# Gate products from float32r parts, front banks two and two, and low-rank weights filled up with zeros

## The chip, the cores and the metric

The kernel runs on one core of a Trainium2 chip. Its time is the device time of one execution, in microseconds (us). Before the change it was 1590.78 us, the median of 3 runs (1585.95 to 1590.83). The engines are TensorE (PE, with PEld for its weight loads), VectorE (DVE), ScalarE (ACT), GpSimd (POOL) and SyncE (SP), which issues most transfers.

## The reference

One encoder layer over 256 tokens of width 1024, all in float32. Only what bears on the change is shown.

```python
p = x @ w_in[l]                                   # 1024 x 10560
hq, hf_f, hf_b, hi, hog, prw, gate_a, gate_b = _split(p, IN_SPLITS)
o_a = _hgrn2_branch(hq, hf_f, hf_b, hi, hog, ...)
o_b, v_raw = _rwkv7_branch(prw, ...)              # inside:
#   w = -softplus(-(w0[d] + tanh(wl_d) @ w_up[d])) - 0.5     for d in 0, 1   (64 x 1024 each)
#   a = sigmoid(a0 + a_lo @ a_up)                                            (64 x 1024)
#   then a recurrence over the 256 tokens, forwards and backwards, 16 heads of 64
merged = sigmoid(gate_a) * (o_a @ proj_a[l]) + sigmoid(gate_b) * (o_b @ proj_b[l])
x = _layernorm(DN_ALPHA * x + merged @ w_out[l], ln1_g[l], ln1_b[l])
x = _layernorm(DN_ALPHA * x + _moe(x, ...), ln2_g[l], ln2_b[l])   # 32 experts, top 4, 12 MB each
```

## The kernel before, in words

The program has a front (all up to the first layer norm and the choice of experts) and the experts' stage, which goes through all 32 experts and streams 1 MB pieces of their weights through a ring of tiles.

In the front, the input is loaded and transposed to `X` (channels on partitions, 8 tiles of 256 tokens). `dense_parts` (L129 to L157) makes one 256-column part of a product with a weight matrix: two transfers of 512 rows into a tile `wt` of a pool of three (L136), then for each 128 rows and each half of the columns a matmul of 128x256 into one bank `bank_d` (L154). With a plain moving operand that is 16 float32 products. With a pair of operands (`mov` a tuple) each piece of `wt` is split first (`split`, L112): ScalarE rounds it to float32r (`wh`, L113), VectorE subtracts (`wl`, L114), and three float32r products wh·hi, wl·hi, wh·lo stand for each float32 one. Before the change only the three projections after the branches (proj_b, proj_a, w_out) use pairs.

The branches run in four quarters of 256 columns. Four generators are interleaved by `interleave` (L377) by their running cost: `dense_stream` (the input columns of a quarter, at the end the eight gate parts), `prepare_stream` (`rwkv_prepare`: per quarter the low-rank products L472 and L479, decays, scores L546, and `inverse`), `mix_stream` (the other branch) and `run_stream` (`rwkv_run`: eight steps per quarter, each of which needs the one before: L685, copy `gs`, L696, masked copy into `W`, L710, ScalarE's copy into `W`, L102). `yield ("need", ...)` makes a generator wait until another has reached a point. The tile framework's scheduler then sets the order on each engine, within what the program's order, the banks and the pools allow; each engine works off its own instructions in that order.

The eight banks of the matmul memory are given out by name in L98: three to dense products ("d"), one to preparation ("p"), two to the chain ("c"), one to the mix ("h"), one to outputs ("y").

`gate_part` (L912) makes a gate part with `dense_parts` on `X`, applies a tanh (L916) and calls `fetch` (L955), which issues the next early loads of expert weights once their places are free (`want`, L966). Early loads follow a fixed list, "llsseellpprrrppqqr". The "r" places are four 8 KB slots per partition: `X`, `obT`, `oaT` and one that stays free until the first "r" load. `split_biases` (L283) loads expert biases and splits them on ScalarE and VectorE beside the gate parts.

In a pair of heads (`pair`, L465) the low-rank weights are `wup` (the two directions on partitions 0 to 63 and 64 to 127) and `aup` (64 partitions), loaded once per quarter. Their products contract over 64 partitions.

Of the kernel before, what the change touches and what calls it, by code (L numbers as in the profile page):

```python
# [8 lines left out]
F32 = mybir.dt.float32  # L9
# [7 lines left out]
P = 128  # L17
S = 256
D = 1024
KT = 8  # L20
# [28 lines left out]
def tile_encoder(ctx: ExitStack, tc: tile.TileContext, A, out):  # L49
# [47 lines left out]

    bd, bs, bc, bh, by = (lambda t=t, n=n: bank(t, n) for t, n in (("d", 3), ("p", 1), ("c", 2), ("h", 1), ("y", 1)))  # L98

# [6 lines left out]
    late = ctx.enter_context(tc.tile_pool(name="late", bufs=1, side="right"))  # L106
    X = late.tile([P, KT, S], F32, name="xT0", tag="r", bufs=4)
    obT = late.tile([P, KT, S], F32, name="obT", tag="r", bufs=4)
    oaT = late.tile([P, KT, S], F32, name="oaT", tag="r", bufs=4)
# [209 lines left out]

    lora = fc.tile([P, 3, S], F32, name="lora")  # L320
    b = lora1
    shift(lora[:, 0, :], b[:, :S], "muw")
# [10 lines left out]
    def dense_stream(rw, tmp, hp):  # L333
        for c in range(4):
            yield ("at", c * QUARTER)
            yield ("need", f"pair{c - 1}")
            yield from rwkv_columns(c, rw, tmp)
            yield ("at", c * QUARTER + 45)
            yield ("need", f"mix{c - 1}")
            yield from hgrn_in(c, hp)  # L340
        yield ("at", 4 * QUARTER)
        yield ("need", "pair3")
        for t_ in ("A", "B"):
            g = late.tile([P, 2, 512], F32, name="gate2", tag=t_)
            yield from gate_part(C_GB + (512 if t_ == "B" else 0), [g[:, 0], g[:, 1]])
        yield ("need", "inv3")
        done.add("e")
        for n, t_ in enumerate(("kt", "k0", "sq", "sg")):
            yield from gate_part(C_GA + 256 * n, [tmp.tile([P, 512], F32, name="gate", tag=t_)])
            split_biases(tmp, n)  # L350
        done.add("gates")
# [65 lines left out]
    def rwkv_prepare(qi, rw, tmp):  # L417
# [8 lines left out]
        cq = slice(256 * qi, 256 * qi + 256)  # L426
        wup = tmp.tile([P, 256], F32, name="wup")
        nc.scalar.dma_start(out=wup, in_=A["rw_w_up"][0].rearrange("a l n -> (a l) n")[:, cq])
        aup = tmp.tile([64, 256], F32, name="aup")
        nc.scalar.dma_start(out=aup, in_=A["rw_a_up"][0][:, cq])  # L430
        KB = late.tile([P, 2, 2, S], F32, name="KB", tag="B")
# [33 lines left out]
        def pair(r):  # L465
# [5 lines left out]
            for d in range(2):  # L471
                T.matmul(b[:, d * S:(d + 1) * S], lhsT=wup[64 * d:64 * d + 64, cj],  # L472
                         rhs=lora[64 * d:64 * d + 64, 0, :], start=True, stop=True)
                SC.activation(sg[:, d, :], b[:, d * S:(d + 1) * S], AF.Tanh, scale=0.5,
                              bias=col(hm, "w0", 8 * d + j))
            V.tensor_scalar(sg, sg, 0.5, 0.5, op0=OP.mult, op1=OP.add)
            at = tmp.tile([P, S], F32, name="at")
            b = bs()
            T.matmul(b[:, :S], lhsT=aup[:, cj], rhs=lora[:64, 1, :], start=True, stop=True)  # L479
            sigmoid(at, b[:, :S], col(hm, "a0", j))  # L480
# [431 lines left out]
    def gate_part(w, tiles):  # L912
        for n, g in enumerate(tiles):
            b = yield from dense_parts(w_in, w + 256 * n, X)
            fetch()
            SC.activation(g, b, AF.Tanh, scale=0.5)  # L916
            gates.append(g)
# [37 lines left out]
    def fetch(n=None):  # L955
# [4 lines left out]
        for _ in range(n):  # L960
            i = len(ahead)
            if i >= order.index("b"):
# [3 lines left out]
            want = dict(l="run2" if m < 2 else "run3", s="ring", e="e", p="runs" if m < NA - 2 else "m", q="m",  # L966
                        r=("gates", "gates", "ob", "oa")[m % 4])[k]
            if want not in done:
# [3 lines left out]

    with tc.tile_pool(name="rw", bufs=1) as rw:
        W = rw.tile([P, NW, 2, 4, 64], F32, name="W")
# [510 lines left out]
```

## Time and profile before

| | |
|---|---|
| median of 3 runs | 1590.78 us |
| profiled execution | 1591.12 us (span 1589.3 us) |
| mean granted TensorE clock | 0.981 |
| TensorE busy | 1455.9 us (92% of the span), 11331 matmul records |
| VectorE busy | 591.2 us (37%) |
| ScalarE busy | 374.4 us (24%) |
| transfers | 467.36 MB, 294 GB/s over the span |

The span is one execution from its first to its last instruction; busy times are sums over instructions, and matmul records may overlap. A float32 matmul of this kernel stands as two records of L154 (664 products of the input, 1328 records). The front ends at about 640 us, and the rest is the experts' stage.

### The profile page before, as it was taken

The page shows a single profiled execution, that of the slowest core. Times are in us where ns is not written, and L with a number is a line of the kernel's source. Part 1 is how long each engine was busy: PE and PEld are TensorE (multiplying, and loading weights), DVE is VectorE, ACT ScalarE, POOL GpSimd, SP SyncE. Part 2 cuts the span into 40 slices and gives each one's busy share as a digit, 9 for nine tenths or more (in the row PEclk, how much of TensorE's full clock was granted, in tenths as well). Part 3 has the DMA queues.
Part 4 walks back from the last instruction along what each step waited for, and adds up shares of the span by engine and source line. Part 5 has one row for each costly group of instructions (what it writes and reads, how often), then busy time and mean ns, then how long its engine had stood idle before and what let it go on. Part 6 is the DMA issues. An engine that isn't in the chain of part 4 may idle for free. (4 is left out here: it accounts for less than half of the span.)

```text
span 1589.3 us, 27117 instructions
## 1 busy us (share of the span) xinstructions
PE 1455.9 (92%) x11331; PEld 796.7 (50%) x11331; DVE 591.2 (37%) x1539; ACT 374.4 (24%) x983; POOL 95.0 (6%) x142
## 2 busy tenths in 40 slices
PE   8989989989988999999999999889999988988985
PEld 7667667667666897444444433244434323322321
DVE  4685885985983465112111111121112111111113
ACT  2426335335335243211111111101111100100100
POOL 0310210210210000000000000000000000000000
PEclk9999999999999999999999999989899999999998
DMA  6322322322344786799999999999999999999995
GB/s 190 108 69 68 86 72 67 86 74 70 99 140 134 262 311 241 305 419 415 418 417 416 417 418 416 417 418 416 416 418 418 415 418 417 416 417 418 416 419 208
DMA packets 133981, 467.36 MB, mean 294 GB/s; under 512 B 9544, under 2 KB 66780, under 8 KB 101084
## 3 DMA queue, kind: packets, MB, share of 16 engines
q1 hardware_dynamic: 129280, 460.88, 74.5%
q10 hardware_dynamic: 4572, 4.68, 0.9%
q8 instruction: 91, 1.49, 0.4%
q14 instruction: 38, 0.31, 0.1%
HBM read 464.48 MB, written 1.05 MB: 293 GB/s over the span
## 5 line engine op out<-in xcount | busy, mean ns | idle before, releaser
L154 PE MATMUL bank_d<-xT,wt 128*128 128x256 f32 x1200 | 311.5, 398 | 0.4 <-DMA wt<-in_w_in_dram 0.4
L154 PEld LDWEIGHTS bank_d<-xT,wt 128*128 128x128 f32 x1200 | 217.4, 193 | 39.8 <-issue 6.2
L1238 DVE SCALAR_TENSOR_TENSOR yl<-ypb,slotg,yh 128x512 fp32r<-128x512 f32 x32 | 24.0, 751 | 483.2 <-ACT yh L1237 460.1
L1202 PE MATMUL hpb<-ring_l,xg 128*64 128x512 f32 x416 | 98.7, 602 | 4.7 <-DMA ring_l<-in_moe_w_dram 4.7
L1202 PE MATMUL hpb<-ring_p,xg 128*64 128x512 f32 x416 | 98.5, 598 | 2.4 <-DMA ring_p<-in_moe_w_dram 2.4
L1184 DVE TENSOR_SCALAR ot<-tpb 128x256 fp32r<-128x256 f32 x32 | 13.6, 425 | 233.9 <-ACT tpb L1183 233.9
L1202 PE MATMUL hpb<-ring_r,xg 128*64 128x512 f32 x408 | 96.3, 598 | 4.4 <-DMA ring_r<-in_moe_w_dram 4.4
L1237 ACT ACTIVATE yh<-ypb,slotg 128x512 fp32r<-128x512 f32 x32 | 22.0, 689 | 309.1 <-PE ypb L1232 309.1
L1163 PE MATMUL tpb<-oh,x 128*128 128x256 f32 (+1 forms) x288 | 65.1, 369 | 4.2 <-ACT xg L1168 3.2
L1183 ACT ACTIVATE tpb<-tpb 128x256 f32<-128x256 f32 x32 | 11.8, 370 | 235.3 <-PE tpb L1181 232.1
L1163 PEld LDWEIGHTS tpb<-oh,x 128*128 128x128 f32 x288 | 48.0, 190 | 35.6 <-DVE glu L1214 17.9
L1149 POOL TENSOR_TENSOR ohg<-oh,gate 128x512 f32<-128x512 f32 (+1 forms) x9 | 8.6, 952 | 867.6 <-PE tpb L1181 849.8
L1202 PEld LDWEIGHTS hpb<-ring_l,xg 128*64 128x64 f32 x416 | 29.0, 138 | 56.7 <-issue 40.6
L1202 PEld LDWEIGHTS hpb<-ring_r,xg 128*64 128x64 f32 x408 | 28.1, 136 | 54.7 <-issue 40.2
L1202 PEld LDWEIGHTS hpb<-ring_p,xg 128*64 128x64 f32 x416 | 27.8, 136 | 51.8 <-issue 42.5
L1232 PE MATMUL ypb<-ring_l,aT 128*64 128x512 f32 x208 | 48.8, 597 | 5.0 <-DMA ring_l<-in_moe_w_dram 5.0
L1232 PE MATMUL ypb<-ring_r,aT 128*64 128x512 f32 x200 | 47.3, 598 | 6.4 <-DMA ring_r<-in_moe_w_dram 6.4
L1202 PE MATMUL hpb<-ring_q,xg 128*64 128x512 f32 x200 | 47.2, 597 | 4.5 <-DMA ring_q<-in_moe_w_dram 4.5
L1232 PE MATMUL ypb<-ring_p,aT 128*64 128x512 f32 x192 | 45.0, 599 | 6.9 <-DMA ring_p<-in_moe_w_dram 6.9
L1202 PE MATMUL hpb<-ring_s,xg 128*64 128x512 f32 x208 | 49.2, 598 | 2.2 <-DMA ring_s<-in_moe_w_dram 2.2
L1216 ACT ACTIVATE sgm<-glu 128x256 f32<-128x256 f32 x64 | 26.7, 418 | 102.6 <-DVE glu L1214 102.6
L1202 PE MATMUL hpb<-ring_e,xg 128*64 128x512 f32 x208 | 48.6, 598 | 1.5 <-DMA ring_e<-in_moe_w_dram 1.5
(332 smaller groups left out, 2214.5 us busy)
## 6 DMA issues: line engine op xcount, KB each, us to landing
ring_l<-in_moe_w_dram SPq DMA_DIRECT2D x78, 1024.0 KB
ring_p<-in_moe_w_dram SPq DMA_DIRECT2D x76, 1024.0 KB
ring_r<-in_moe_w_dram SPq DMA_DIRECT2D x76, 1024.0 KB
wt<-in_w_in_dram SPq DMA_DIRECT2D x84, 512.0 KB
ring_s<-in_moe_w_dram SPq DMA_DIRECT2D x40, 1024.0 KB
ring_e<-in_moe_w_dram SPq DMA_DIRECT2D x38, 1024.0 KB
ring_q<-in_moe_w_dram SPq DMA_DIRECT2D x38, 1024.0 KB
ring_b<-in_moe_w_dram SPq DMA_DIRECT2D x38, 1024.0 KB
```

Source lines behind the costliest of these rows:

```text
L154: T.matmul(o, lhsT=lhsT, rhs=rhs, start=n == 0, stop=n == last)
L1149: G.tensor_tensor(out=ohg[:, :, :n], in0=oh[:, :, :n], in1=gate[:, :, es[0]:es[0] + n].unsqueeze(3).to_broadcast([P, 2, n, 64]), op=OP.mult)
L1163: T.matmul(b[:, kk * 256:kk * 256 + ne * 64], lhsT=x1[t][:, n * P:(n + 1) * P], rhs=oh[:, t, :ne].rearrange("p e s -> p (e s)"), start=t = ...
L1183: SC.activation(b[:, :S], b[:, :S], AF.Copy, accum_out=sg)
L1184: V.tensor_scalar(ot, b[:, :S], 0.0, None, op0=OP.is_gt)
L1202: T.matmul(self.hbs[cc][64 * j:64 * j + 64, :], lhsT=self.xg[:, k, self.ei, :], rhs=self.w1[k][:, c0:c0 + 512], start=False, stop=k == KT - 1)
L1216: SC.activation(sgm[cc], glu[cc], AF.Sigmoid, scale=1.702)
L1232: T.matmul(yb[64 * j:64 * j + 64, :], lhsT=self.aT[:, k % 4, 64 * (k // 4):64 * (k // 4) + 64], rhs=self.w2[k][:, j * 512:(j + 1) * 512], ...
L1237: SC.activation(yh, yb, AF.Copy, scale=self.sg)
L1238: V.scalar_tensor_tensor(out=yl, in0=yb, scalar=self.sg, in1=yh.bitcast(F32), op0=OP.mult, op1=OP.subtract)
```

## The change

Four edits, apart from places that follow from them.

1. `X` is split once into `Xh` and `Xl` (float32r), in `dense_stream` after the last pair. `Xh` takes the fourth "r" slot; `Xl` and the weight parts of the gates live in a new pool `gx` (three buffers for the parts). `gate_part` hands the pair to `dense_parts`. The first "r" load now waits for "split" instead of "gates", and takes the slot of `X`.
2. The banks: "d" has two instead of three, "p" two instead of one.
3. The low-rank weights lie in one tile `ups` of 128 partitions, with zeros where a direction or `aup` has no rows, and `lora` has zeros in the unused half; all products contract over 128 partitions. Three transfers per quarter load it.
4. Three memsets at the start write those zeros.

```diff
-    bd, bs, bc, bh, by = (lambda t=t, n=n: bank(t, n) for t, n in (("d", 3), ("p", 1), ("c", 2), ("h", 1), ("y", 1)))
+    bd, bs, bc, bh, by = (lambda t=t, n=n: bank(t, n) for t, n in (("d", 2), ("p", 2), ("c", 2), ("h", 1), ("y", 1)))
...
     X = late.tile([P, KT, S], F32, name="xT0", tag="r", bufs=4)
+    Xh = late.tile([P, KT, S], F32R, name="xh", tag="r", bufs=4)
...
     lora = fc.tile([P, 3, S], F32, name="lora")
+    V.memset(lora[64:128, 1, :], 0.0)
+    ups = fc.tile([P, 3, 256], F32, name="ups")
+    V.memset(ups[64:128, 0:3:2, :], 0.0)
+    V.memset(ups[0:64, 1, :], 0.0)
...
         yield ("need", "pair3")
+
+        Xl = gx.tile([P, KT, S], F32R, name="xl", bufs=1)
+        for k in range(0, KT, 2):
+            split(Xh[:, k:k + 2], Xl[:, k:k + 2], X[:, k:k + 2], V)
+            yield 1
+        box["parts"] = Xh, Xl
+        done.add("split")
...
-        wup = tmp.tile([P, 256], F32, name="wup")
-        nc.scalar.dma_start(out=wup, in_=A["rw_w_up"][0].rearrange("a l n -> (a l) n")[:, cq])
-        aup = tmp.tile([64, 256], F32, name="aup")
-        nc.scalar.dma_start(out=aup, in_=A["rw_a_up"][0][:, cq])
+        for d in range(2):
+            nc.scalar.dma_start(out=ups[64 * d:64 * d + 64, d], in_=A["rw_w_up"][0][d][:, cq])
+        nc.scalar.dma_start(out=ups[0:64, 2], in_=A["rw_a_up"][0][:, cq])
...
-                T.matmul(b[:, d * S:(d + 1) * S], lhsT=wup[64 * d:64 * d + 64, cj],
-                         rhs=lora[64 * d:64 * d + 64, 0, :], start=True, stop=True)
+                T.matmul(b[:, d * S:(d + 1) * S], lhsT=ups[:, d, cj], rhs=lora[:, 0, :], start=True, stop=True)
...
-            T.matmul(b[:, :S], lhsT=aup[:, cj], rhs=lora[:64, 1, :], start=True, stop=True)
+            T.matmul(b[:, :S], lhsT=ups[:, 2, cj], rhs=lora[:, 1, :], start=True, stop=True)
...
-            b = yield from dense_parts(w_in, w + 256 * n, X)
+            b = yield from dense_parts(w_in, w + 256 * n, box["parts"])
...
-                        r=("gates", "gates", "ob", "oa")[m % 4])[k]
+                        r=("split", "gates", "ob", "oa")[m % 4])[k]
...
-    with tc.tile_pool(name="rw", bufs=1) as rw:
+    with tc.tile_pool(name="rw", bufs=1) as rw, tc.tile_pool(name="gx", bufs=3) as gx:
+        hlp[0] = gx
```

Line numbers of the new program are one higher from L112 on (L154 is L155, L195 is L196) and about eleven higher in `rwkv_prepare` and behind it (L472 is L483, L479 is L489, L546 is L556).

The scheduler orders the front anew. TensorE at the start of the program, before: `x_tok` is the input, `prm` the parameter rows, `xT_75` is `X`.

```order
L188 MATMUL bank_d<-ident,x_tok 128x128 x16
L154 MATMUL bank_d<-xT_75,wt 128x256 x24
L195 MATMUL bank_p<-ident,prm 128x116
L154 MATMUL bank_d<-xT_75,wt 128x256 x40
L443 MATMUL bank_p<-blk,sq 128x2 x4
```

And after the change:

```order
L189 MATMUL bank_d<-ident,x_tok 128x128 x12
L196 MATMUL bank_p<-ident,prm 128x116
L189 MATMUL bank_d<-ident,x_tok 128x128 x4
L155 MATMUL bank_d<-xT_75,wt 128x256 x64
L454 MATMUL bank_p<-blk,sq 128x2 x4
```

The transposition of the parameter rows has moved from behind the first 24 products to a place ahead of all of them.

TensorE in the first pair of the first quarter, before: `vT` is transposed, `wup` and `aup` are the low-rank weights, `sqb` and `BK` belong to the same pair.

```order
L461 MATMUL bank_p<-ident,vT 128x128
L154 MATMUL bank_d<-xT_75,wt 128x256 x2
L461 MATMUL bank_p<-ident,vT 128x128 x3
L154 MATMUL bank_d<-xT_75,wt 128x256 x2
L472 MATMUL bank_p<-lora,wup 128x256
L154 MATMUL bank_d<-xT_75,wt 128x256 x2
L472 MATMUL bank_p<-lora,wup 128x256
L154 MATMUL bank_d<-xT_75,wt 128x256 x2
L479 MATMUL bank_p<-lora,aup 128x256
L154 MATMUL bank_d<-xT_75,wt 128x256 x12
```

And after the change:

```order
L472 MATMUL bank_p<-ident,vT 128x128
L483 MATMUL bank_p<-lora,ups 128x256
L155 MATMUL bank_d<-xT_75,wt 128x256
L472 MATMUL bank_p<-ident,vT 128x128 x3
L483 MATMUL bank_p<-lora,ups 128x256
L155 MATMUL bank_d<-xT_75,wt 128x256
L489 MATMUL bank_p<-lora,ups 128x256
L155 MATMUL bank_d<-xT_75,wt 128x256 x9
```

The three low-rank products stand closer together, with one dense product instead of two between them; each still has other work on both sides.

ScalarE in the last steps of the last quarter's chain, before: `W<-bank_c` carries the state to the next step, `W<-vt` writes values, `gate` is a gate part's tanh.

```order
L102 ACTIVATE W<-bank_c 64x2x128 x2
L102 ACTIVATE W<-vt 32x2x64 x4
L916 ACTIVATE gate_5628<-bank_d 128x512
L102 ACTIVATE W<-bank_c 64x2x128 x2
L916 ACTIVATE gate_5628<-bank_d 128x512
L102 ACTIVATE W<-bank_c 64x2x128 x2
L916 ACTIVATE gate<-bank_d 128x512 x3
```

And after the change:

```order
L926 ACTIVATE gate_5778<-bank_d 128x512
L102 ACTIVATE W<-bank_c 64x2x128 x2
L114 ACTIVATE wh<-wt 128x512
L292 ACTIVATE bias<-BK 128x768
L114 ACTIVATE wh<-wt 128x512 x2
L294 ACTIVATE bias<-BK 64x768
L114 ACTIVATE wh<-wt 128x512
L926 ACTIVATE gate_5778<-bank_d 128x512
L114 ACTIVATE wh<-wt 128x512
L102 ACTIVATE W<-bank_c 64x2x128 x2
L114 ACTIVATE wh<-wt 128x512 x3
```

Between two copies of the state ScalarE now has five roundings of weights, and a bias split that stood earlier.

## Rows read from the trace of the kernel before

**Rows 1.** The page's slices of the span: 40 slices of 39.7 us each.
```profile
GB/s 190 108 69 68 86 72 67 86 74 70 99 140 134 262 311 241 305 419 415 418 417 416 417 418 416 417 418 416 416 418 418 415 418 417 416 417 418 416 419 208
```

**Rows 2.** Windows: us; PE, PEld, DVE, ACT, POOL busy (instructions); PEclk, DMA share, GB/s.
```profile
20.00:60.00 40.00, 38.49 (x186) 31.22 (x186) 21.96 (x64) 14.96 (x41) 4.10 (x6) 1.00 0.50 146
180.00:220.00 40.00, 33.21 (x352) 25.88 (x350) 39.11 (x95) 14.04 (x34) 9.44 (x11) 1.00 0.36 102
440.00:500.00 60.00, 47.96 (x865) 36.26 (x854) 42.16 (x105) 27.22 (x85) 8.07 (x13) 0.94 0.45 148
500.00:533.80 33.80, 33.80 (x341) 26.51 (x342) 4.53 (x14) 8.17 (x22) 0.29 (x1) 1.00 0.54 168
533.80:550.60 16.80, 16.80 (x88) 14.99 (x89) 11.26 (x46) 5.35 (x11) 0.00 (x0) 1.00 0.72 254
550.60:640.00 89.40, 84.94 (x660) 78.27 (x660) 53.65 (x118) 36.13 (x61) 0.19 (x1) 0.96 0.79 284
700.00:1570.00 870.00, 809.17 (x4018) 309.26 (x4016) 135.65 (x318) 102.25 (x240) 6.91 (x7) 0.99 1.01 415
```

**Rows 3.** L154 alone: windows of PE; then ns min/median/max, first and last start.
```profile
22.00:37.00 15.00, 15.00 (x71) 1.00 0.61 177
554.00:569.00 15.00, 15.00 (x133) 1.00 0.88 321
...
L154 PE MATMUL bank_d<-xT,wt x1200: 379/379/796, 9.1 to 548.7; 128*128 128x256 f32 x172
L154 PE MATMUL bank_d<-obh,wh x64: 276/276/365, 550.6 to 574.3; 128*128 128x256 f32 x64
```

**Rows 4.** Timeline of PE: start us, us, instruction; two stretches.
```profile
47.57 0.70 PE L472 MATMUL bank_p<-lora,wup 64*128 64x256 f32 x2
48.19 1.13 PE L154 MATMUL bank_d<-xT,wt 128*128 128x256 f32 x4
49.25 0.70 PE L472 MATMUL bank_p<-lora,wup 64*128 64x256 f32 x2
...
542.86 0.60 PE L741 MATMUL bank_c<-lora,gup 128*128 128x256 f32 x2
543.29 1.46 PE L154 MATMUL bank_d<-xT,wt 128*128 128x256 f32 x6
544.59 0.59 PE L741 MATMUL bank_c<-lora,gup 128*128 128x256 f32 x2
```

**Rows 5.** Timeline of PE and ACT's queue at the start; ACT's queue from 10 to 11.
```profile
6.05 3.17 PE L188 MATMUL bank_d<-ident,x_tok 128*128 128x128 f32 x15 [1.04 <-DMA x_tok<-in_x_dram]
9.06 10.54 PE L154 MATMUL bank_d<-xT,wt 128*128 128x256 f32 x48
19.43 0.26 PE L195 MATMUL bank_p<-ident,prm 116*128 116x116 f32 x1
20.12 1.10 PE L154 MATMUL bank_d<-xT,wt 128*128 128x256 f32 x4 [0.42 <-DMA wt<-in_w_in_dram]
...
9.74 0.28 ACTq L182 DMA_DIRECT2D prm<-in_ln_b_dram  x1
...
q10 hardware_dynamic: 12, 0.00, 1.4%
```

**Rows 6.** Groups (busy us, mean ns); waits to 620 us (total, times, longest); PE's timeline.
```profile
L113 ACT ACTIVATE wh<-wt 128x512 fp32r<-128x512 f32 x48 | 29.2, 629 | 32.3 <-PE bank_d L154 14.4 <-DMA wt<-in_proj_a_dram 10.7 <-DMA wt<-in_w_out_dram 3.2
L114 DVE TENSOR_TENSOR wl<-wt,wh 128x512 fp32r<-128x512 f32 x48 | 31.9, 687 | 15.8 <-ACT wh L113 15.8
...
ACT bias L291 <- DMA BK<-in_moe_b_dram: 23.2, 4, 8.0
ACT wh L113 <- DMA wt<-in_proj_a_dram: 10.7, 8, 3.2
PE bank_p L546 <- DVE L L553: 5.1, 4, 1.6
...
450.67 0.66 PE L827 MATMUL bank_h<-QQ,KS 128*32 128x32 f32 x32 [3.84 <-ACT KS L102]
```

## The prediction

> **What bounds the kernel now.** I read first the page's slices [rows 1]: from the 18th slice on, at 675 us, the DMA rate stands at 415 to 419 GB/s until the last slice. That is the experts' stage, which streams the expert weights. The view by windows gives the same for 700 to 1570 us: DMA share 1.01, 415 GB/s, TensorE 809 of 870 us [rows 2]. Nothing there is changed, the loads keep their order, and only a fixed list of them is fetched early. So this stage starts when the front has ended, takes as long as before, and a microsecond gained or lost ahead of 640 us moves the end by one microsecond.
>
> The front is then read window by window [rows 2]. From 20 to 60 us TensorE works 38.5 of 40 us, VectorE 22. From 180 to 220 us, where a quarter's pairs and inverse stand, VectorE works 39.1 of 40 and TensorE only 33.2. From 440 to 500 us no engine is full (TensorE 48.0 of 60, VectorE 42.2, ScalarE 27.2): steps wait for each other. From 500 to 550.6 us TensorE is busy without a gap (33.8 of 33.8 and 16.8 of 16.8), with the last steps of the recurrent chain and the gate products between them. From 550.6 to 640 it works 84.9 of 89.4 on the three projections. So work taken from TensorE counts in the first and in the fourth of these stretches, and is hidden in the second.
>
> **The change part by part.**
>
> *Gate products.* The eight gate parts hold 16 products of 128x256 each, 128 in all. A float32 product stands as two records. In 15 us of nothing but these the windows count 71 records of 0.379 us [rows 3]; records that reach over an edge count too, so the spacing is (15 + 0.379)/71 = 0.2166 us and a product 0.433. The projections already use float32r parts: 133 records of 0.276 us in 15 us, (15 + 0.276)/133 = 0.1149 us each. Three of them make a gate product: 0.345 us. The change gives back 128 x (0.433 - 0.345) = 11.3 us of TensorE's time. In the new order a step of the last chain has 48 float32r records beside it (5.5 us) where three quarters of a gate part stood (12 products, 5.2 us). The steps thus stay about as long, but each takes a whole gate part along, and 132 records (15.2 us) are left behind the chain's last output instead of 32 products (13.9 us). The saving must therefore appear in the stretch before that output. I take it whole, since TensorE is the full engine there.
>
> What it adds lies on ScalarE and VectorE: 4 + 32 roundings of 128x512 on ScalarE (0.629 us each, 22.6 us) and as many subtractions on VectorE (0.687 us, 24.7 us) [rows 6]. From 440 to 550.6 us these two are busy for 40.7 and 58.0 of 110.6 us [rows 2], so they fit. The four splits of x are placed by the order in the second quarter, far from need. The risk is the queue: the roundings stand on ScalarE between the copies that carry the state from step to step. Bounds: if the x split and the first gate part stood in series in the path, 8 x 0.629 + 8 x 0.687 = +10.5 us; if the new order took away all of TensorE's idle time from 440 to 500 us, -12.0. I take 0, by the nearest row: after 500 us TensorE waits for nothing.
>
> *Low-rank products.* Wup and aup products (24: 16 and 8) use 64 rows of the array. Such a product takes 47.57 to 48.19 = 0.62 us, and the four records behind it 48.19 to 49.25 = 1.06 us, where 4 x 0.2166 = 0.87 would do [rows 4]. A 128-row product of the same columns, from 542.86 to 543.29, takes 0.43, and the six records behind it 1.30, exactly 6 x 0.2166. So a 64-row product costs 0.19 + 0.19 = 0.38 us more than a filled one, 24 of them 9.1 us. The Trainium skill ("TensorEngine Tiling (Array Packing)", Key Properties) says that changing the tiling mode drains TensorE; the rows agree, with 0.38 us per pair of changes. The same notes ("TensorE: Matmul & The Clock Gate", Why this matters for your kernels) advise the opposite for small contractions: slices at different partitions, so that they run at once. By that rule the filled form would lose 0.43 us per pair of directions, 0.9 us in the first quarter, and the sum would be 1581.5; the rows show the two products 1.7 us apart, so no such overlap is there to lose. Six of the 24 lie in the first quarter, where TensorE is full: -2.3 us. The other 18 lie where VectorE is full; the nearest row is 180 to 220 us, and I take 0 for them. Bounds: 0 and -9.1. The three memsets stand before the first x arrives and cost nothing.
>
> *The start.* Before, the transposition of the parameter rows (L195) stood behind the first 24 products. In the new order it stands ahead of the last four transpositions of x, and so ahead of all products, because the second "p" bank is free. It waits for 15 small transfers. The last is issued at 9.74 us [rows 5]; in the window from 10 to 11 us twelve packets of that queue still move. I estimate its landing at 11.8 us, between 11 and 13. Then follow 0.26 us for it and 4 x 0.21 for the transpositions, and products start at 12.9 instead of 9.06: +3.8. The pause from 19.43 to 20.12 goes: -0.7. Net +3.1, bounds 0 and +5. From 20 to 60 us TensorE is the full engine [rows 2], so its lateness is passed on.
>
> *Banks two and two.* TensorE's waits for a reader of the single "p" bank sum to 5.1 us in the largest row [rows 6], and that is the most to win. With two "d" banks instead of three, a product may run only one product (6.9 us) ahead of its reader; ScalarE stands up to 8.0 us in four waits for the bias transfers (23.2 us in all) [rows 6], so up to 4 x 1.1 = 4.4 us could be lost. TensorE's 3.84 us of idle time ahead of L827 at 450.67 come from ScalarE, late in this way. I take 0.
>
> **Sum.** -11.3 - 2.3 + 3.1 = -10.5 us. The profiled execution took 1591.1 us (span 1589.3), 0.3 above the median of the runs, so 1580.6, told as 1580.5.
>
> **The rivals.**
> 1. *The drain counts everywhere* (the rule named above, taken in full). If TensorE is late in all quarters, because what VectorE waits for comes from it, the other 18 low-rank products count too: -6.8 more, 1573.8. For it: in each pair VectorE's work comes behind these products. Against: VectorE's 39.1 of 40 us [rows 2].
> 2. *The chain is the bound.* If the last chain keeps its length from 440 to 533.8 us, since its copies now share ScalarE with roundings, then only the 32 products left behind it shrink, by 32 x 0.088 = 2.8 us: 1591.1 - 2.8 - 2.3 + 3.1 = 1589.1. For it: the stretch from 440 to 500, where no engine is full. Against: from 500 us on TensorE has no gap.
> 3. *ScalarE waits for weights, with the chain behind it: slower.* A rounding needs its weight tile, and ScalarE works in order. In the projections such waits are 10.7 us in 8 [rows 6], 1.34 each, and cover nothing but the next rounding. With the gates, 16 tiles come this way, and state copies stand behind them; if each wait is passed on, +21.4 us: 1602. It outweighs the gain from 0.66 us per tile on. For it: the DMA share there is 0.54 to 0.72, with expert loads in the same queue. Against: three tiles are in flight, and a tile now comes free after the split, not after the product.
>
> **How the numbers follow.** Forecast 0.50 (1575 to 1586), rival 1 0.15, rival 2 0.22, rival 3 0.13. The measurement can tell 0.3%, 4.8 us, so faster means below 1586.0 and slower above 1595.6. Faster: 0.50 + 0.15 + 0.03 of rival 2 = 0.68. Slower: 0.10 of rival 3. Same: 0.22. The range 1571 to 1592 holds the forecast, most of rival 1 and rival 2, and leaves rival 3 out; it covers the open terms of the start and of the banks.
>
> **What would show it.** In the new profile: the first product at about 13 us; gate records spaced 0.115 us; low-rank products of 128 rows with 0.43 us to the next record; the first projection product about 10 us earlier than 550.6; the same 415 GB/s after that. Wrong would be: ScalarE waiting for the weight transfers or for bias transfers ahead of state copies, with TensorE idle from 500 to 540 us; or larger gaps in the middle quarters.

## The result, and the profile after

The changed kernel takes 1570.12 us, the median of 4 runs (1567.42 to 1573.84), beside 1590.8 us for the kernel before: a ratio of 0.9876 with a 95% interval of 0.9844 to 0.9908, or -19.7 us (-24.8 to -14.6). The forecast was -10.5. The direction held; the gain is twice as large, the median lies 0.9 us below the low end of the range (by the ratio it is 1571.1, at its very edge), and most of it does not come from where I had looked for it. The span of the profiled execution is 1569.9 us.

The experts' stage is as it was. The page's slices, clock above and rate below, to be held against [rows 1]:

```profile
PEclk9999999999999999999999999989899999999998
GB/s 168 98 78 81 86 74 81 100 59 82 110 123 198 289 293 219 386 415 417 419 415 416 418 417 415 418 417 415 418 417 416 417 418 418 415 418 417 416 419 211
```

415 to 419 GB/s again from the 18th slice on, and the 17th has 386 where it had 305. From the start of the last group of router products (L1065; L1054 before) to the end it took 959.6 us before and 957.3 now. So the front has to be read. The windows of the kernel after, in the columns of [rows 2], the last two cut at the first projection product (535.3 us; 550.6 before):

```profile
20.00:60.00 40.00, 38.81 (x193) 32.45 (x191) 18.35 (x50) 15.14 (x41) 0.49 (x1) 1.00 0.51 145
180.00:220.00 40.00, 35.47 (x576) 28.52 (x575) 38.77 (x115) 14.80 (x36) 6.43 (x9) 0.96 0.29 84
440.00:500.00 60.00, 50.07 (x776) 43.14 (x774) 38.61 (x95) 39.15 (x112) 7.97 (x13) 0.91 0.43 141
500.00:535.30 35.30, 34.47 (x341) 32.76 (x341) 23.69 (x68) 16.91 (x31) 0.19 (x1) 0.95 0.82 274
535.30:612.60 77.30, 74.20 (x618) 72.37 (x617) 49.69 (x89) 33.30 (x56) 0.00 (x0) 0.98 0.74 260
```

TensorE is still not full from 440 to 500 us, it has gaps from 500 us on where it had none, and the granted clock is 0.91 and 0.95 where it was 0.94 and 1.00. The gate products, the part from which I expected most, run in the stretch that looks worse than before.

A fixed window compares different work in two kernels. Cut at events of the program instead (the first low-rank product of a quarter, the first projection product, the last group of router products), the profiled executions divide like this. "Work" is TensorE's busy time less what the lower clock cost, "clock" is that cost (in windows of 1 us, the sum of one minus the granted clock), "idle" the rest of the stretch, "turns" the number of places in TensorE's timeline where two neighbouring records have different rows*columns of the array:

| kernel | to quarter 1 | quarters 1 to 3 = work + clock + idle (turns) | quarter 4 to first projection = work + clock + idle | projections |
|---|---|---|---|---|
| before | 47.6 | 342.2 = 305.8 + 8.5 + 27.9 (295) | 160.8 = 141.4 + 3.4 + 16.0 | 79.1 |
| zeros only | 48.8 | 334.5 = 300.3 + 6.8 + 27.4 (266) | 163.0 = 139.7 + 6.8 + 16.5 | 79.5 |
| gates only | 47.9 | 339.5 = 306.2 + 6.8 + 26.5 (297) | 162.4 = 129.8 + 12.3 + 20.3 | 76.8 |
| dense banks only | 54.1 | 342.0 = 305.7 + 8.5 + 27.8 (295) | 164.0 = 141.1 + 5.1 + 17.8 | 79.9 |
| banks only | 51.3 | 325.1 = 299.6 + 1.7 + 23.8 (257) | 153.0 = 142.4 + 0.0 + 10.6 | 83.4 |
| banks and zeros | 52.7 | 325.8 = 296.8 + 5.1 + 23.9 (240) | 152.7 = 141.2 + 3.4 + 8.1 | 79.1 |
| full change | 51.2 | 327.7 = 297.2 + 10.2 + 20.3 (244) | 156.5 = 132.4 + 8.8 + 15.2 | 77.3 |

(The five in the middle are experiments, below. Each row is one profiled execution.) Of the 19.4 us by which the span fell, 14.5 come from quarters 1 to 3, 4.3 from the fourth with the gates, 1.8 from the projections and 2.3 from the rest; 3.6 are lost at the start.

The places that the prediction named, after. The start (TensorE's timeline; compare [rows 5]):

```profile
12.51 0.43 PE L196 MATMUL bank_p<-ident,prm 116*128 116x116 f32 x1 [3.79 <-DMA rwt<-in_router_w_dram]
12.73 1.06 PE L189 MATMUL bank_d<-ident,x_tok 128*128 128x128 f32 x4
```

Products start at 13.59 us (forecast about 13). The low-rank products, now of 128 rows (compare [rows 4]):

```profile
51.17 0.60 PE L483 MATMUL bank_p<-lora,ups 128*128 128x256 f32 x2
51.61 0.59 PE L155 MATMUL bank_d<-xT,wt 128*128 128x256 f32 x2
52.07 0.55 PE L472 MATMUL bank_p<-ident,vT 128*128 128x128 f32 x3
52.45 0.60 PE L483 MATMUL bank_p<-lora,ups 128*128 128x256 f32 x2
52.89 0.59 PE L155 MATMUL bank_d<-xT,wt 128*128 128x256 f32 x2
```

51.17 to 51.61 is 0.44 us (forecast 0.43, before 0.62). And gate records, 21 of them from one of these rows to the other:

```profile
476.01 0.28 PE L155 MATMUL bank_d<-xl,wh 128*128 128x256 f32 x1
...
478.51 0.28 PE L155 MATMUL bank_d<-xl,wh 128*128 128x256 f32 x1
```

(478.51 - 476.01)/21 = 0.119 us each (forecast 0.115). So every price of a single operation was right. What was wrong is where they count.

### The profile page after: what moved, and what is told of

The parts are those of the page before. It is cut to its first block, busy times and chain, and to the rows that moved or that the text cites. A ratio compares the mean times of both kernels' runs of the same rounds, so it can differ in the third digit from the quotient of the medians.

```text
span 1569.9 us, 27470 instructions
## 1 busy us (share of the span) xinstructions
PE 1441.8 (92%) x11459; PEld 806.8 (51%) x11459; DVE 602.1 (38%) x1578; ACT 395.1 (25%) x1019; POOL 90.2 (6%) x142
## 5 line engine op out<-in xcount | busy, mean ns | idle before, releaser
L155 PE MATMUL bank_d<-xT,wt 128*128 128x256 f32 x944 | 238.7, 395 | 0.4 <-ACT pad L102 0.4
L155 PEld LDWEIGHTS bank_d<-xT,wt 128*128 128x128 f32 x944 | 173.5, 193 | 27.9 <-issue 1.5
L115 DVE TENSOR_TENSOR wl<-wt,wh 128x512 fp32r<-128x512 f32 x80 | 54.1, 688 | 33.2 <-ACT wh L114 31.6
L1174 PEld LDWEIGHTS tpb<-oh,x 128*128 128x128 f32 x288 | 48.0, 190 | 35.5 <-DVE glu L1225 17.8
L114 ACT ACTIVATE wh<-wt 128x512 fp32r<-128x512 f32 x80 | 48.9, 628 | 46.9 <-PE bank_d L155 26.3
L1213 PEld LDWEIGHTS hpb<-ring_r,xg 128*64 128x64 f32 x408 | 28.1, 137 | 54.7 <-issue 40.2
L1213 PEld LDWEIGHTS hpb<-ring_p,xg 128*64 128x64 f32 x416 | 27.9, 137 | 51.4 <-issue 42.5
L1243 PE MATMUL ypb<-ring_l,aT 128*64 128x512 f32 x208 | 48.8, 597 | 4.9 <-DMA ring_l<-in_moe_w_dram 4.9
```

The source lines that it names most:

```text
L114: SC.activation(hi, src, AF.Copy)
L115: eng.tensor_tensor(out=lo, in0=src, in1=hi.bitcast(F32), op=OP.subtract)
L155: T.matmul(o, lhsT=lhsT, rhs=rhs, start=n == 0, stop=n == last)
L1174: T.matmul(b[:, kk * 256:kk * 256 + ne * 64], lhsT=x1[t][:, n * P:(n + 1) * P], rhs=oh[:, t, :ne].rearrange("p e s -> p (e s)"), start=t = ...
L1213: T.matmul(self.hbs[cc][64 * j:64 * j + 64, :], lhsT=self.xg[:, k, self.ei, :], rhs=self.w1[k][:, c0:c0 + 512], start=False, stop=k == KT - 1)
L1243: T.matmul(yb[64 * j:64 * j + 64, :], lhsT=self.aT[:, k % 4, 64 * (k // 4):64 * (k // 4) + 64], rhs=self.w2[k][:, j * 512:(j + 1) * 512], ...
```

## Experiments

All are compared with the kernel before by the ratio of runs on the same chip in the same session. The us behind a ratio are worked out from it and that session's median of before.

**Zeros alone.** Only edits 3 and 4. The order on TensorE stays the same, row for row.

```diff
-                T.matmul(..., lhsT=wup[64 * d:64 * d + 64, cj], rhs=lora[64 * d:64 * d + 64, 0, :], ...)
+                T.matmul(..., lhsT=ups[:, d, cj], rhs=lora[:, 0, :], ...)
...
-            T.matmul(b[:, :S], lhsT=aup[:, cj], rhs=lora[:64, 1, :], ...)
+            T.matmul(b[:, :S], lhsT=ups[:, 2, cj], rhs=lora[:, 1, :], ...)
```

> The kernel before, with only the low-rank weights and inputs filled up to 128 rows. Every engine keeps its order of work. Theory A (the prediction's): only the 6 products of the first quarter count, 6 x 0.38 = -2.3 us, 1588.5. Theory B (rival 1: the cost of the 64-row form counts in all quarters): 24 x 0.38 = -9.1 us, 1581.7. B is also what the two profiles suggest, where TensorE's busy time in each middle quarter fell by 2.4 to 3.2 us.

Measured: 1583.14 us, ratio 0.9964 (0.9942 to 0.9987), -5.7 us (-9.2 to -2.1). TensorE's work in quarters 1 to 3 fell by 5.5 us, and by 1.7 in the fourth: 7.2 for 24 products, 0.30 each where I had 0.38. B is right in that they count in all quarters. The 29 turns that went are 0.19 us each.

**Gates alone.** Only edit 1.

```diff
-            b = yield from dense_parts(w_in, w + 256 * n, X)
+            b = yield from dense_parts(w_in, w + 256 * n, box["parts"])
```

> The kernel before, with only the gate products from float32r parts (and X split). Theory A (the prediction's): 128 x 0.088 = -11.3 us, 1579.5, gained ahead of the first projection product. Theory C (the chain of the last quarter is the bound, as in rival 2): only what stands behind the chain shrinks, -2.8 us, 1588. The profile of the full change points to C: from the fourth quarter's first low-rank product to the first projection product it took 156.5 us against 160.8, and 2.3 of these 4.3 are owed to the low-rank products.

Measured: 1583.33 us, ratio 0.9957 (0.9940 to 0.9975), -6.8 us (-9.5 to -4.0): between the two. But the stretch with the gates did not get shorter: 162.4 us against 160.8. Work fell by 11.6 there, as forecast, and came back as 8.9 of clock and 4.3 of idle time. In this execution what was gained lies elsewhere: 2.7 in quarters 1 to 3, 2.3 in the projections, 3.0 behind them; why was not tested. The granted clocks of all runs say the same of the clock: 0.978 on average in these 12 runs, 0.982 in the 23 of the kernel before. Span times one minus the clock makes that 34.1 and 28.2 us lost; what is left of the span fell by 12.2 us.

**Banks alone.** Only edit 2.

```diff
-... (("d", 3), ("p", 1), ("c", 2), ("h", 1), ("y", 1)))
+... (("d", 2), ("p", 2), ("c", 2), ("h", 1), ("y", 1)))
```

> The kernel before, with only two banks each for the dense products and for preparation. Theory A (the prediction's): the start is 3.1 us later and the rest even, 1594. Theory D (the second preparation bank takes away TensorE's idle time in the middle quarters): the start 4 us later, and about 3.6 us of idle time gained in each of the second and third quarters as in the profile of the full change, so -3 us, 1587.5.

Measured: 1573.66 us, ratio 0.9897 (0.9872 to 0.9923), -16.4 us (-20.3 to -12.2). The term that I had put at 0 is the largest of all, and outside its bounds. Theory D has the right part and too small a price. The windows over quarters 1 to 3 (first low-rank product to the fourth quarter's first), before and then with the banks alone:

```profile
47.57:389.80 342.23, 314.31 (x4382) 235.41 (x4381) 259.53 (x689) 151.39 (x464) 60.42 (x79) 0.98 0.28 78
```

```profile
51.32:376.41 325.09, 301.30 (x4354) 232.37 (x4353) 249.57 (x690) 150.37 (x462) 57.43 (x79) 0.99 0.29 83
```

TensorE is busy for 13 us less with the same work to do (the records differ by 28, at the cuts), and that is the surprise: three quarters of the gain are not gaps that closed but busy time that went. Of these 13 us, 6.8 are clock; how far that holds for other runs is told in the part on the prediction.

**Start mended.** The changed kernel, with one line more:

```diff
     for k in range(0, KT, 2):
-        b = bd()
+        b = bd() if k < 4 else bc()
```

> The changed kernel, with the last two groups of transpositions of x in the chain's banks instead of the dense ones, so that the first two dense banks are not waited for and the transposition of the parameter rows stands behind the first 24 products again, as before. Theory A (the start's lateness is passed on to the end): products start at 9.1 instead of 13.6 us and the end comes about 4 us earlier than in the changed kernel, 1566. Theory E (the first quarter's later waits take the lateness up): within 1 us of the changed kernel, 1570.

Measured: 1570.01 us, ratio 0.9867 (0.9839 to 0.9895): no difference from the changed kernel that this can tell. Products start at 9.26 us, and yet the first low-rank product comes at 50.79 instead of 51.17. A row of TensorE's timeline shows where the 4.3 us went:

```profile
23.96 19.22 PE L155 MATMUL bank_d<-xT,wt 128*128 128x256 f32 x80 [3.34 <-ACT sh_t L309]
```

TensorE stands for 3.34 us until ScalarE has read the first of the two dense banks; that read needs a value out of the parameter rows, whose transposition is now late again. The granted clock is 0.57 from 24 to 28 us, behind this pause. With two dense banks the parameter rows are waited for either way, before the products or between them. So theory E holds, though what takes the lateness up is the pair of dense banks, not a wait in the first quarter.

**One preparation bank, two dense banks.** This splits the bank edit.

```diff
-... (("d", 3), ("p", 1), ...
+... (("d", 2), ("p", 1), ...
```

> The kernel before with two dense banks instead of three and one preparation bank as before (one bank stays unused). Theory H (the second preparation bank brings all of the gain, the lost dense bank costs the start): products start at 13.6 us and the end is about 4 us later than before, 1592. Theory I (fewer dense products ahead of their readers leave fillers for the stretches where TensorE is idle): faster than before by 5 us or more, below 1583.

Measured: 1597.67 us, ratio 1.0036 (1.0022 to 1.0050), +5.7 us. Theory H: the lost dense bank costs 5.7 us (in the profile the first low-rank product is 6.5 us late), and the second preparation bank is worth the difference to the kernel with both, 0.9897 - 1.0036, about -22 us. The transposition of the parameter rows moves ahead of the products in this kernel too, which has one "p" bank.

**Banks and zeros.** The full change less the gates' edit (the diff of the gates alone, undone).

> The changed kernel without its first edit: gate products in float32 again, banks two and two, low-rank weights filled up. Theory A (each part keeps its own gain): 1588.5 - 16.4 (banks only) - 5.4 (zeros only) = 1567 and the gates' 5.2 on top would have made the full change 1562; as that was 1570, at least one gain is lost in company. Theory F (the gates' gain is lost once the chain is short: ScalarE's bias splits wait for their transfers inside the chain, VectorE's state copies stand behind them): 1567 to 1569, not slower than the full change. Theory G (the low-rank gain is lost with two preparation banks): 1573, as banks only, and the gates bring 3.

Measured: 1570.18 us, ratio 0.9861 (0.9839 to 0.9884), -22.1 us. The full change has 0.9876 (0.9844 to 0.9908). So in this company the gates' edit gives nothing that can be measured, and the profile says why: 8.8 us less work in its stretch, 5.4 more of clock and 7.1 more of idle time, 156.5 us against 152.7. Whether the zeros still count beside two "p" banks is not settled: the ratios of this and of banks alone have overlapping intervals, and the 2.8 us of work that went from quarters 1 to 3 came back as clock. The nine profiled kernels with both, here and below, take 324.9 to 327.7 us for quarters 1 to 3, and banks alone takes 325.1, so nothing in that stretch shows that they do.

**Where TensorE waits in the gates' stretch.** No run of its own, but the reading on which the next ones rest. Timelines of the full change from 492 to 501 us, ScalarE first, then VectorE, then TensorE, and the windows behind them:

```profile
497.28 0.84 ACT L292 ACTIVATE bias<-BK 128x768 bf16<-128x768 f32 x1 [5.17 <-DMA BK<-in_moe_b_dram]
```

```profile
498.16 0.96 DVE L293 TENSOR_TENSOR BK<-BK,bias 128x768 f32<-128x768 f32 x1 [5.32 <-ACT bias L292]
499.03 0.68 DVE L115 TENSOR_TENSOR wl<-wt,wh 128x512 fp32r<-128x512 f32 x1
499.64 0.28 DVE L104 COPY gs<-bank_c 128x128 f32<-128x128 f32 x1
```

```profile
499.98 0.43 PE L706 MATMUL bank_c<-gs,Y 32*32 32x64 f32 x16 [3.53 <-DVE gs L104]
```

```profile
492.00:501.00 9.00, 5.47 (x70) 4.95 (x70) 3.50 (x6) 3.47 (x6) 0.00 (x0) 1.00 0.34 89
501.00:505.00 4.00, 4.00 (x44) 3.49 (x43) 2.55 (x5) 1.82 (x4) 0.00 (x0) 0.57 0.59 163
```

Read upwards: TensorE waits 3.53 us for the chain's `gs`. VectorE could have copied it at 494.8, when L695 (494.39) had ended, but stood at L293 for the bias group, because ScalarE stood at L292 for the transfer. TensorE was idle for 3.53 of the 9 us, and in the next one the granted clock is 0.57, so it is at 1.2 GHz for most of it. This was theory F; rival J held the splits of the gate weights themselves guilty.

**Bias loads early.**

```diff
+        fgs = [load_biases(BK, 0), load_biases(f12[:, :768], 1), load_biases(f12[:, 768:1536], 2)]
         for n, t_ in enumerate(("kt", "k0", "sq", "sg")):
             yield from gate_part(...)
-            split_biases(tmp, n)
+            split_biases(fgs[n], n)
+            if n == 0: fgs.append(load_biases(BK, 3))
```

> The changed kernel with the four bias loads issued ahead of the last four gate parts, into tiles that are free by then, instead of one after each part into one tile; the splits stay. Theory F (the waits for bias transfers in the chain, 5.2 and 2.1 us on ScalarE, make TensorE idle for 8.8 us and then run at the lower clock): the stretch from the fourth quarter's first low-rank product to the first projection product falls from 156.5 to about 148, the end to 1562. Rival J (the roundings and subtractions themselves delay the state's copies): 155 to 157, the end within 2 us of the changed kernel.

Measured: 1574.47 us, ratio 0.9894 (0.9876 to 0.9911): no better than the full change, and both theories missed (the stretch took 159.5 us). The scheduler, seeing the data early, moved the splits early too, into the stretch where VectorE is full: ScalarE waited for the transfers there (17.6 us in 3 waits), the first chain step of the last quarter came at 458.2 us instead of 445.0, with half the clock from 450 to 464. The late steps did become short (the state's copies on ScalarE 5.8 to 8.2 us apart, against 10.8 and 12.9 in the full change). Inconclusive on the cause.

**The same, with the subtractions on GpSimd.**

```diff
-                    split(wh, wl, wq, V)
+                    split(wh, wl, wq, G if hlp[0] is box.get("gx") else V)
```

> As the kernel with early bias loads, and the subtractions of the gates' weight parts on GpSimd instead of VectorE (32 of 128x512). Theory F: VectorE is not what is late once the bias waits are gone: within 3 us of that kernel, 1560 to 1565. Rival J: VectorE's 32 x 0.69 = 22 us leave the queue of the state's copies, 5 us or more faster than that kernel. If GpSimd takes much longer for one than VectorE's 0.69 us, the float32r products wait for it and the run is slower than 1568.

Measured: 1573.93 us, ratio 0.9894 (0.9872 to 0.9915): as the kernel above, within the 3 us of theory F, though both are far from its 1560. VectorE had 32 instructions less and the end did not move. Its busy time in the stretch fell by 9.3 us only (119.8 to 110.5), where 22 had been expected, and one subtraction took GpSimd 1.32 us:

```profile
L115 POOL TENSOR_TENSOR wl<-wt,wh 128x512 fp32r<-128x512 f32 x32 | 41.9, 1319 | 46.9 <-ACT wh L114 40.7 <-issue 3.4 <-PE bank_c L714 1.9
```

(The view of groups by line: busy us and mean ns of one, then the idle time ahead of them.)

**Bias loads and splits behind the chain** (with the mended start):

```diff
                 b = dense(wp, 256 * g, (hi, lo))
+                if g % 2 == 0: fg = load_biases(mg, 2 * which + g // 2)
+                else: split_biases(fg, 2 * which + g // 2)
```

> The kernel with the mended start, and the four bias loads and splits moved behind the chain, beside the first two projections (a tile of a pool that opens there). So nothing on ScalarE or VectorE waits for a bias transfer while the chain runs. Theory F (the bias waits in the chain ate the gates' gain): the stretch from the fourth quarter's first low-rank product to the first projection product falls from 156.4 to 147 to 149 us, the projections take 1 us more, the end is at 1562. Rival J (the roundings and subtractions themselves delay the chain's copies): the stretch stays at 155 or more, the end at 1569.

Measured: 1582.34 us, ratio 0.9947 (0.9931 to 0.9962). The end is worse, but the stretch in question speaks against rival J: with the waits gone from the chain, quarter 4 to the first projection takes 144.2 us, against 156.3 in the kernel with the mended start, with the same splits of weights on the same engines and no lower clock at all. The work of the bias splits left the stretch too (0.84 us for each of two roundings and 0.96 for each of two subtractions in a group), so the run shows the price of waits and bias splits together; that the waits are the larger part is read from the timelines above. Two windows, up to the first projection product and from there to the router:

```profile
376.79:520.98 144.19, 135.21 (x1946) 114.39 (x1944) 112.10 (x305) 74.71 (x194) 19.69 (x28) 1.00 0.51 162
520.98:621.78 100.80, 81.43 (x618) 78.08 (x617) 56.43 (x97) 39.55 (x64) 0.00 (x0) 0.90 0.66 216
```

The 12 us gained and 11 more are lost in the projections, where the waits now stand (view of waits, 500 to 625 us; total, times, longest):

```profile
ACT bias L295 <- DMA fg<-in_moe_b_dram: 28.5, 4, 10.3
DVE fg L296 <- ACT bias L295: 26.1, 4, 10.2
...
PE bank_d L155 <- ACT wh L114: 14.1, 3, 8.4
```

My "1 us more" for the projections was wrong by 22: ScalarE waits up to 10.3 us for a bias transfer there, beside the expert loads, and roundings stand behind it.

**The same, with float32 gates** (the diff of the gates alone, undone in the kernel above).

> As the run before, with the gate products in float32 again. Theory F: the gates' parts are worth 4 to 8 us once the bias waits are gone, so this is slower than the run before, 1566 to 1570. Rival J: the gates' parts bring nothing or cost 2 to 4 us in any company, so this is equal or faster, 1562 to 1566.

Measured: 1594.52 us, ratio 1.0025 (1.0011 to 1.0038), slower by 12 us. In the profiled executions, 16.5 us apart, the larger part is the projections (113.7 us against 100.8), where the bias waits meet this kernel harder; in the stretch with the gates it is 149.8 against 144.2. So without bias waits in the chain the gates' parts are worth 5.6 us there: 6.7 of work and 1.7 of clock less, 2.8 of idle time more. That is theory F in the stretch; its time for the whole kernel, like J's, was far off. Held against the kernels with the biases in the chain, moving them shortened the stretch by 12.1 us with float32r gates (156.3 to 144.2) and by 2.9 with float32 ones (152.7 in banks and zeros, whose start is another, to 149.8).

**Splits left out.** The reverse test of rival J.

```diff
-                    wh, wl = new tiles; split(wh, wl, wq, V)
+                    if len(hlp) > 1: wh, wl = hlp[1]
+                    else: ...; split(wh, wl, wq, V); hlp.append((wh, wl))
```

> The changed kernel with 31 of the 32 splits of gate weights left out: all gate products use the parts of the first piece, so the gates' values are not the reference's. TensorE's products and their order of magnitude stay, ScalarE and VectorE are spared 31 x 0.63 and 31 x 0.69 us, and the bias waits stay in the chain. Rival J: the stretch from the fourth quarter's first low-rank product to the first projection product falls from 156.5 to 148 or less, 1562. Theory F: 153 to 156, 1567 to 1570.

Measured: 1577.91 us, ratio 0.9917 (0.9899 to 0.9934), slower than the full change by its ratio (0.9876), though the intervals touch. The stretch took 163.4 us, 7 more than with the splits. That misses both numbers, and J by its sign. The view of waits, 370 to 545 us:

```profile
ACT bias L297 <- DMA BK<-in_moe_b_dram: 23.6, 4, 10.5
...
PE bank_c L700 <- ACT W L102: 9.6, 1, 9.6
...
PE bank_c L669 <- ACT Z L102: 5.4, 1, 5.4
```

ScalarE, relieved of the roundings, waited longer for the bias transfers (23.6 us in 4 waits, 13.0 in the full change), with the state's copies behind it. Timelines of ScalarE and its queue tell whether it came sooner or the transfers later. The last group, issue and end of the wait, with the splits left out:

```profile
478.06 1.14 ACTq L295 DMA_DIRECT2D BK<-in_moe_b_dram  x2
493.83 0.84 ACT L297 ACTIVATE bias<-BK 128x768 bf16<-128x768 f32 x1 [10.45 <-DMA BK<-in_moe_b_dram]
```

In the full change the issue that belongs to the wait of 5.17 us shown above:

```profile
488.31 1.10 ACTq L290 DMA_DIRECT2D BK<-in_moe_b_dram  x2
```

From the issue to the end of the wait it is 15.8 us against 9.0, and ScalarE began to wait 5.3 us behind the issue against 3.8. So it did not come sooner; the transfers landed later, while the core moved 297 GB/s (478 to 494 us) against 143 (488 to 498 us). That the other loads held them up is not shown. As the waits grew, this run is no clean test of J.

**Loads early, splits held late.** The version to which this points: the three loads early as above, and each split tied on ScalarE behind the tanh of its gate part, so that the scheduler can't pull it forward.

```diff
-            split_biases(fgs[n], n)
+            with tc.issue_after(last[0].ins):     # last[0]: the part's tanh
+                split_biases(fgs[n], n)
```

> The changed kernel with the mended start, the first three bias loads issued early (as in the kernel with early bias loads) and each split held behind the tanh of one of the last four gate parts, so that it stands behind the chain's last copy on ScalarE and its data has long landed; the fourth load follows the first split. Theory F (the bias waits ate the gates' gain in the chain, and moved along with the splits in the two kernels that shifted them): the fourth quarter's first low-rank product to the first projection product takes 144 to 147 us as in the kernel with late biases, the projections 77 to 80 as in the changed kernel, the end is at 1557 to 1561, faster than all others. Rival K (the fourth transfer lands late and ScalarE waits with roundings behind it): 4 to 8 us more, 1563 to 1567. Rival J (the splits of weights are what delays the chain): 155 us for that stretch, 1568.

Measured: 1565.44 us, ratio 0.9847 (0.9823 to 0.9872), -24.3 us (-28.1 to -20.3). It has the lowest ratio of all kernels run, though its interval overlaps that of the full change. No wait for a bias transfer is left in the front. Three windows: quarter 4 to the chain's last output, from there to the first projection product, the projections:

```profile
376.50:498.33 121.83, 115.21 (x1758) 94.50 (x1756) 95.20 (x249) 63.31 (x175) 19.48 (x27) 0.99 0.47 146
498.33:527.98 29.65, 24.85 (x190) 23.19 (x189) 21.40 (x61) 14.31 (x25) 0.19 (x1) 0.88 0.65 221
527.98:606.43 78.45, 75.96 (x616) 74.11 (x616) 53.77 (x93) 37.04 (x61) 0.00 (x0) 0.98 0.75 266
```

The first took 134.2 us in the full change, so 12.4 us are gained. The second took 22.3, so 7.4 are given back: the four splits now stand between the last gate parts' roundings, and TensorE is idle for 4.8 us of that stretch and at the lower clock for part of it (0.88). Theory F's 144 to 147 us came out as 151.5, its 1557 to 1561 as 1565. That lies in rival K's 1563 to 1567, but the late fourth transfer that K names is not in the trace.

## Why the prediction was right, and where it was wrong

*What bounds the kernel.* Right: the experts' stage kept its length within 2.3 us, and the front's gain arrived at the end.

*Banks two and two: taken as 0, bounds -5.1 to +4.4; measured -16.4.* This is the step that failed. I bounded the second "p" bank by TensorE's waits for a reader of the single one, 5.1 us in the largest row [rows 6], "and that is the most to win". It was not even all of these waits: the same view has another row for a reader of that bank.

```profile
PE bank_p L546 <- DVE bon L492: 3.2, 4, 1.1
```

Neither row is left in banks only. And such a row counts only the time in which TensorE stood at that bank. It leaves out what the scheduler does so that TensorE won't stand there: with one bank it puts dense products between two preparation products. Each such place is two turns, for which I had a price in hand (0.38 us per pair, from [rows 4]) and which I applied to 24 products instead of to every turn in the order. In quarters 1 to 3 the second bank (dense banks only against banks only) takes 16.9 us away: 6.1 of work for 38 fewer turns, 0.16 each; 6.8 of clock; 4.0 of idle time (the clock's part does not hold over the runs, see below). The other half of the edit I had nearly right: the lost dense bank costs 5.7 us, with a bound of 4.4.

The Trainium skill ("TensorEngine Tiling (Array Packing)", Key Properties) says that a change of tiling mode drains TensorE. The runs agree, with 0.16 to 0.19 us of work per turn. The Trainium skill ("TensorE: Matmul & The Clock Gate", A second HAM failure mode: psum-queue depth-cycling) describes a kernel whose short pauses at its banks bring the lower clock. The runs do not show that of these banks: in quarters 1 to 3 the clock cost 6.8 to 8.5 us in the four profiled kernels with one preparation bank, and 1.7 to 10.2, 6.3 on average, in the ten with two.

*Low-rank products: taken as -2.3; measured -5.7 alone.* The size per product was near (0.30 us for 0.38), the place was wrong. "The other 18 lie where VectorE is full", and I took 0 for them: they counted, as rival 1 said, at least in the kernel without the other edits. VectorE's 39.1 of 40 us hold in the window that I chose, but over quarters 1 to 3 it is busy for 259.5 of 342.2 us, and TensorE for 314.3. I read a whole quarter from its fullest 40 us.

*Gate products: taken as -11.3, whole.* The work that went is 8.8 to 11.6 us, as forecast. The step that failed is "I take it whole, since TensorE is the full engine there", and with it, for the splits, "I take 0, by the nearest row". The prediction's own sign of error, ScalarE waiting for bias transfers ahead of state copies, is what came: I had counted 23.2 us of these waits before, and used them for the banks alone. They cost less beside float32 gate products: with their splits they are worth 2.9 us of the stretch there and 12.1 beside float32r ones. In the full change they reach the chain through VectorE's queue, and its gates' stretch is 3.8 us longer than with float32 gates: 7.1 of idle time and 5.4 of clock more, 8.8 of work less. Without them the edit is worth 5.6 us there, half of what I took.

*The start: taken as +3.1.* First product at 13.59 us, 3.6 us late at the first low-rank product: the size was right. The reason that I gave ("because the second p bank is free") was wrong: the order moves with two dense banks and one "p" bank just as well, and mending it doesn't bring the time back.

*The sum.* -10.5 came out as -19.7 because one term at 0 was -16 and the gates' term did not arrive. Alone the three parts give -16.4, -5.7 and -6.8, together -28.9, and in company -19.7. Banks and zeros together measured -22.1, as much as their two alone, so it is the gates' part that shows no gain in company. That the direction held and the time came to the edge of the range is luck: the largest term failed, and one that was put at nothing stood in for it.

*The rivals.* Rival 1 (1573.8) named a true mechanism and came nearest in time, with the banks' part, the largest, not in it. Rival 2 (the chain bounds the gates' stretch) was right about that stretch. Rival 3 had the queue right, ScalarE waiting with state copies behind it, and the wrong transfer: biases, not weights.

That fewer turns, less idle time and a higher clock together make the 16.9 us is read from single profiled executions. For the clock every run has its granted mean: span times one minus that mean is 25.2 us on average in the six runs of banks only and 28.2 in the 23 of the kernel before, 3.0 apart. In the two profiled executions it is 20.4 (0.987 over 1570.8 us) and 30.2 (0.981 over 1589.3 us). So the clock's 6.8 is in good part the luck of one execution; without the clock the mean span fell by 12.4 us.

## What to carry to other kernels

Price a change of banks by the order that it lets the scheduler make, not by the waits that the trace shows at the bank: count the places where the array's shape turns, before and after, and give each its price. Here that would have given some 7 us (38 turns at 0.19, by [rows 4]) of the 17 in quarters 1 to 3; the rest showed only in a run. When filler work of a latency-bound chain gets shorter, look first for whatever else stands in the queues of the chain's engines and waits for a transfer; here it cost 2.9 us of the stretch beside the long filler and 12.1 beside the short one. And when such a wait is moved, hold its consumer back as well as starting its load early, or the scheduler puts the wait in another place.

## What had not been expected of the hardware

A turn of the array's shape costs TensorE 0.16 to 0.19 us (38 turns fewer, 6.1 us less work with the second preparation bank; 29 fewer, 5.5 us less with the filled-up products), and the front before, with some 400 of them, spends by that price about 70 us so (an estimate). Stretches at 1.2 GHz (granted clock 0.5) lasted from 3 us to 20 us and stood behind pauses of TensorE such as the one of 3.53 us above; up to 640 us they cost 15.4 us before the change, 6.8 in banks only, and 22.2 in the full change and with the gates alone. The bias transfers of 256 and 128 KB made ScalarE wait for up to 13.3 us beside the expert loads (late biases with float32 gates; 8.0 us before the change).
